# Bias tile, mask and lambda of the first attention made during the first feed-forward network, by way of DRAM

## The chip, the cores and the metric

The kernel runs on one core of one Trainium2 chip. The metric is the device time of one launch in microseconds (us), lower is better. Everything is fp32; no matrix product may lose fp32 accuracy, so each large product is made of three single-pass products of operands that are split into a high and a low part (fp32r), which is why TensorE (PE) has three kinds of rows, lines 147 to 149.

## The reference, cut to what matters

A transformer of two blocks on 256 tokens of 1024 features. The first block has two layers; in layer 0 a feed-forward network, then a differential attention, then a second feed-forward network follow each other. Only what feeds the first attention matters here:

```python
lam = exp(sum(lf[0] * lf[1])) - exp(sum(lf[2] * lf[3])) + lambda_init     # a_lambda, four vectors of 64
rel = q_pos[:, None] - k_pos[None, :]
bias = table[t5_bucket(rel)]                                             # rel_bias: 32 buckets x 8 heads
logits = q k^T * scale + bias                                            # two maps m of each of 8 heads
logits = where(rel >= 0, logits, -inf)
p = softmax(logits);  w = p[map 0] - lam * p[map 1];  o = w @ v
o = rms_norm(o, subln_g) * (1 - lambda_init)
```

The bias depends on `rel` alone, so for one head it is a Toeplitz matrix: each row is the row above it, moved by one column. Neither the bias nor `lam` depends on the activations; all they need are the small inputs `rel_bias`, `a_lambda` and a one-hot table `t5` of the bucket of each distance.

## The kernel before, in words

**Weights.** All weights stream from DRAM in chunks of 1 MB, `raw` [128, 2048] (line 105, three buffers, loaded by the DMA queue of SyncE, called SP). ScalarE (ACT) writes the high part `whi` of each half (line 115), VectorE (DVE) the low part `wlo` (line 116), four buffers each; PE multiplies them with the activations (`hi`, `lo`). A second stream `araw` (line 355, two buffers, the same queue) feeds the modulation vectors, whose products DVE makes by itself (line 358) in the background, one step every so many chunks.

**Order.** The Python text is written in program order; a scheduler then decides the order in which each engine gets its instructions. Each engine takes its own list strictly in order. Tiles that share an address wait for one another through semaphores, and so do the buffers of a tile.

**Stages around the change.** First the keys and values of a memory (`w_xk`, `w_xv`). Then the first feed-forward network (`ffn(0, ...)`): 22 chunks `ffn_in`, each giving two products, a SiLU on ACT and a split, and then 11 chunks `ffn_out`. Then the first attention: four groups `g` of two heads, in each the projections `a_q`, `a_k` and `a_v` of the next chunk and then `a_head` of two heads. GpSimd (POOL) does little: sums of squares (line 193) in the second half of the feed-forward network and some memsets.

**The bias tile.** `TB` [128, 8, 256] holds the negated bias of a head, mask included, as one Toeplitz tile; line 523 adds it to the logits. Before, it is made inside the attention, when group 0 has its projections:

```python
pe.matmul(pf, rb, oh, start=True, stop=True)                                       # L582: 8 heads x 384 distances
dve.scalar_tensor_tensor(gneg, pf, -1.0, mrow, op0=ALU.mult, op1=ALU.add)          # L584
for hd in range(8):                                                                # L588: row p is gneg moved by p
    sync.dma_start(out=TF[:, hd, :], in_=bass.AP(tensor=s_.tensor, offset=s_.offset,
                                                 ap=[list(s_.ap[0]), [1, 128], [1, 256]]))
a_v(0)
pe.matmul(pb, flip, TF[:, 2 * q:2 * q + 2, :], start=True, stop=True)              # L610, four times
act.activation(TB[:, 2 * q:2 * q + 2, :], pb, AF.Copy)                             # L611
```

Each transfer of line 588 reads one SBUF partition (one head's 384 values) 128 times over, 1 KB each time with the start moved by one value, and writes 128 partitions. The result has its rows in the wrong order, so that a product with a flipped unit matrix turns it round (line 610, plain fp32, two passes each). `nlam` (lines 599 to 605) and `g08` (line 607) are made beside it.

Of the kernel before, what the change touches and what calls it, by code (L numbers as in the profile page):

```python
# [10 lines left out]
F32 = mybir.dt.float32  # L11
# [8 lines left out]
T = 256  # L20
# [10 lines left out]
# ---- columns of the packed per-feature vectors: name -> (first column, count)  # L31
# [22 lines left out]
def forward(ctx: ExitStack, tc: tile.TileContext, io, out, tap=None):  # L54
# [21 lines left out]
    # ---------------------------------------------------------------- constants  # L76
# [15 lines left out]
    # ---------------------------------------------------------------- weights  # L92
    class Weights:
        """Streams [128, 2048] chunks; each gives two pieces split exactly into hi + lo."""
# [5 lines left out]
        def pieces(self, src, n=2048, whole=(), loads=1):  # L100
            """whole: pieces that stay plain fp32, for PE's own (slower) fp32 product."""
# [23 lines left out]
    def after(ref):  # L125
        """keeps background work from running ahead of its place in the queue."""
        return tc.issue_after(ref[0].ins) if ref[0] is not None else nullcontext()
# [17 lines left out]
    def mm3(o, a, b, start, stop):  # L145
        """o += a.T @ b for operands split into (hi, lo)."""
# [4 lines left out]
    def tok(h, k, a=0, b=T):  # L151
        """tokens a .. b of feature tile k."""
        return h[0][:, k, a:b], h[1][:, k, a:b]
# [4 lines left out]
    def split_into(pair_hi, pair_lo, src, func=AF.Copy, **kw):  # L158
        """exact hi + lo of src (an fp32 SBUF tile)."""
# [3 lines left out]
    # ---------------------------------------------------------------- norms  # L163
    class Stat:
        """Sum of squares over the features: tokens on partitions, then 1 / rms again along the row."""
# [7 lines left out]
        def sum(self, sq, first, last_):  # L173
            # the first product also clears the other half of the bank
# [27 lines left out]
        def rstd_after(self, r1):  # L202
            """1 / rms of the rows that r1 scales."""
# [7 lines left out]
    def along_row(r):  # L211
        """[token, 2] -> the same values along the tokens of every partition."""
# [9 lines left out]
    class Norm:  # L222
        """h = (src * a) * r + b in hi + lo, in place of src * a, which the first products take:
        they need no r, which is multiplied into what they give (two more columns carry b)."""
# [21 lines left out]
        def pair(self, p0, p1, keep=None):  # L246
            """two output tiles [128, T] in SBUF; then h is what it should be."""
# [29 lines left out]
    def fm_pair(p0, p1, h):  # L277
        """two feature-major output tiles [128, T]; k outermost."""
# [15 lines left out]
    def proj_fm(W, name, h, consume, c0=0, c1=None, whole=(), h32=None, ahead=None, norm=None, wide=False):  # L294
        """feature-major projection: consume(n, psum) for each output tile n.
        norm: h is still to be scaled; wide: h is only just coming."""
# [334 lines left out]
    if tap:  # L631
        tap("x_attn0", xT)
# [670 lines left out]
```

## Time and profile before

| | |
|---|---|
| device time, three runs | 2295.49, 2296.33, 2296.72 us (median 2296.33) |
| span of the profiled execution, first to last instruction | 2292.8 us |
| profiled span below the median of the runs | 3.6 us |
| mean clock of PE | 0.991 of full speed |
| PE busy | 2235.5 us |

The profile shows one execution; of its time beside the span the record gives nothing more, so that the difference of 3.6 us to the median holds both what lies around the span and what differs between runs. "Idle before" in a row of the trace is the time for which an engine had nothing to do ahead of that instruction, with what ended it. PEld is the loading of PE's stationary operand, SPq the queue of SyncE. Busy shares of PE come from modelled ends of pipelined products, so the time between the starts of two products is a better measure than their durations.

### The profile page before, as it was taken

The page shows a single profiled execution, that of the slowest core. Times are in us where ns is not written, and L with a number is a line of the kernel's source. Part 1 is how long each engine was busy: PE and PEld are TensorE (multiplying, and loading weights), DVE is VectorE, ACT ScalarE, POOL GpSimd, SP SyncE. Part 2 cuts the span into 40 slices and gives each one's busy share as a digit, 9 for nine tenths or more (in the row PEclk, how much of TensorE's full clock was granted, in tenths as well). Part 3 has the DMA queues.
Part 4 walks back from the last instruction along what each step waited for, and adds up shares of the span by engine and source line. Part 5 has one row for each costly group of instructions (what it writes and reads, how often), then busy time and mean ns, then how long its engine had stood idle before and what let it go on. Part 6 is the DMA issues. An engine that isn't in the chain of part 4 may idle for free.

```text
span 2292.8 us, 42711 instructions
## 1 busy us (share of the span) xinstructions
PE 2235.5 (98%) x16756; PEld 2133.5 (93%) x16756; DVE 1739.7 (76%) x3503; ACT 1257.1 (55%) x2389; POOL 72.0 (3%) x75
## 2 busy tenths in 40 slices
PE   8999869999999999999999999999999999999998
PEld 8999858999999999999999999999999999888886
DVE  7877727977877777855699886899668998666665
ACT  5544538644564447644533455545567776555554
POOL 0000100100200010100100000000000000000000
PEclk9999979999999999999999999999999999999999
DMA  9777664677667773455444543245543444555554
GB/s 367 297 295 294 208 138 170 234 299 279 230 266 297 293 292 129 169 202 183 167 164 166 184 181 151 95 184 184 184 166 132 145 148 148 184 190 194 185 185 155
DMA packets 66489, 466.15 MB, mean 203 GB/s; under 512 B 7472, under 2 KB 8944, under 8 KB 10480
## 3 DMA queue, kind: packets, MB, share of 16 engines
q1 hardware_dynamic: 66000, 462.90, 55.4%
q8 instruction: 132, 2.16, 0.4%
q14 instruction: 69, 0.57, 0.1%
q10 hardware_dynamic: 288, 0.52, 0.1%
HBM read 461.26 MB, written 1.05 MB: 202 GB/s over the span
## 4 chain that ended last, share of the span: by engine, by line
PE 90%; DVE 3%; ACT 3%; issue 1%; SPq 1%; DMA 1%; POOL 0%; DVEq 0%; ACTq 0%; POOLq 0%
PE mm L149 22%; PE mm L147 22%; PE mm L148 22%; PE mm L1164 8%; PE lg L1164 8%; PE lg L1114 2%; PE mm L289 2%; SPq L588 1%; PE po L177 1%; DVE wlo L116 1%; ACT whi L115 1%; DMA TF<-gneg 1%; DVE lo L275 0%; DVE lo L238 0%; DVE nt L270 0%
## 5 line engine op out<-in xcount | busy, mean ns | idle before, releaser
L116 DVE TENSOR_TENSOR wlo<-raw,whi 128x1024 fp32r<-128x1024 f32 x696 | 850.1, 1226 | 325.2 <-ACT whi L115 323.7
L115 ACT ACTIVATE whi<-raw 128x1024 fp32r<-128x1024 f32 x696 | 734.3, 1059 | 617.9 <-PE mm L148 411.9
L147 PE MATMUL mm<-hi,whi 128*128 128x256 f32 x3144 | 899.3, 287 | 0.9 <-ACT hi L274 0.6
L149 PE MATMUL mm<-hi,wlo 128*128 128x256 f32 x3144 | 891.7, 284 | 1.4 <-DVE wlo L116 1.1
L148 PE MATMUL mm<-lo,whi 128*128 128x256 f32 x3144 | 886.1, 282 | 0.6 <-DVE lo L275 0.5
L149 PEld LDWEIGHTS mm<-hi,wlo 128*128 128x128 f32 x3144 | 595.4, 189 | 3.0 <-DVE wlo L116 2.7
L148 PEld LDWEIGHTS mm<-lo,whi 128*128 128x128 f32 x3144 | 595.6, 189 | 2.6 <-DVE lo L275 1.2
L147 PEld LDWEIGHTS mm<-hi,whi 128*128 128x128 f32 x3144 | 594.4, 189 | 2.6 <-ACT hi L274 0.8
L149 PE MATMUL mm<-ghi,wlo 128*128 128x256 f32 x704 | 197.7, 281 | 0.0
L147 PE MATMUL mm<-ghi,whi 128*128 128x256 f32 x704 | 197.7, 281 | 0.0
L148 PE MATMUL mm<-glo,whi 128*128 128x256 f32 x704 | 197.7, 281 | 0.0
L358 DVE CUSTOM_DVE_ANT_0 araw<-araw,cb 128x1024 f32<-128x1024 f32 x160 | 190.3, 1218 | 1.0 <-ACT cb L407 1.0
L160 ACT ACTIVATE vph<-S 128x128 fp32r<-128x128 f32 x256 | 77.1, 302 | 133.0 <-PE lg L1164 132.9
L148 PEld LDWEIGHTS mm<-glo,whi 128*128 128x128 f32 x704 | 132.8, 189 | 0.0
L147 PEld LDWEIGHTS mm<-ghi,whi 128*128 128x128 f32 x704 | 132.8, 189 | 0.0
L149 PEld LDWEIGHTS mm<-ghi,wlo 128*128 128x128 f32 x704 | 132.8, 189 | 0.0
L161 DVE TENSOR_TENSOR vpl<-S,vph 128x128 fp32r<-128x128 f32 x256 | 73.5, 288 | 44.3 <-PE lg L1164 44.2
L812 DVE SCALAR_TENSOR_TENSOR cfc<-cf,vec,cfc 128x256 f32<-128x256 f32 x240 | 99.1, 472 | 0.0
L1106 DVE TENSOR_SCALAR ohA<-cst,sel 128x128 f32<-128x128 f32 x256 | 82.2, 342 | 21.8 <-PE lg L1114 20.9
L1164 PE MATMUL mm<-whi,vph 128*128 128x512 f32 x256 | 80.3, 395 | 0.2 <-ACT vph L160 0.2
L1164 PE MATMUL lg<-whi,vpl 128*128 128x512 f32 x256 | 80.5, 395 | 0.0
L1164 PE MATMUL mm<-wlo,vph 128*128 128x512 f32 x256 | 80.5, 395 | 0.0
(387 smaller groups left out, 3279.7 us busy)
## 6 DMA issues: line engine op xcount, KB each, us to landing
raw<-ffn_in SPq DMA_DIRECT2D x88, 1024.0 KB, 4.8
araw<-ada SPq DMA_DIRECT2D x72, 1024.0 KB, 6.8
raw<-peer_u SPq DMA_DIRECT2D x64, 1024.0 KB, 4.8
raw<-peer_v SPq DMA_DIRECT2D x64, 1024.0 KB, 4.8
raw<-ffn_out SPq DMA_DIRECT2D x44, 1024.0 KB, 4.8
araw<-kv_ada SPq DMA_DIRECT2D x8, 1024.0 KB, 6.9
raw<-w_cf SPq DMA_DIRECT2D x8, 1024.0 KB, 4.8
raw<-w_scx SPq DMA_DIRECT2D x8, 1024.0 KB, 4.8
```

Of the source, the lines that this page charges most:

```text
L115: act.activation(hi[:, :m], r, AF.Copy)
L116: last_split[0] = dve.tensor_tensor(lo[:, :m], r, hi[:, :m], op=ALU.subtract)
L147: pe.matmul(o, a[0], b[0], start=start, stop=False)
L148: pe.matmul(o, a[0], b[1], start=False, stop=False)
L149: pe.matmul(o, a[1], b[0], start=False, stop=stop)
L160: act.activation(pair_hi, src, func, **kw)
L161: dve.tensor_tensor(pair_lo, src, pair_hi, op=ALU.subtract)
L289: pe.matmul(o, p[0][:, k * 128:(k + 1) * 128], h32[:, k, :], start=(k == 0), stop=(k == KT - 1))
L358: dve.tensor_tensor_reduce(out=raw[:, i, :], in0=raw[:, i, :], in1=cb, scale=1.0, scalar=0.0, op0=ALU.mult, op1=ALU.add, accum_out=acc[:, ...
L812: dve.scalar_tensor_tensor(o, cf[:, i, j:j + T], w, o, op0=ALU.mult, op1=ALU.add)
L1106: dve.tensor_scalar(A, iota, sel3[:, 0, t:t + 1], sel3[:, 2, t:t + 1], op0=ALU.is_equal, op1=ALU.mult)
L1164: pe.matmul(acc[t][d], lh, rh[:, d * 512:(d + 1) * 512], start=s0, stop=s1)
```

## The change

`TB`, `nlam` and `g08` are made while the first feed-forward network runs, in a generator `prepare_bias` that is moved on at four places: ahead of the network (three small loads, now on POOL's queue, and two memsets), ahead of its chunks 4 and 6, and behind it. The eight transfers from one partition each and the four flips are gone. Instead POOL's queue writes the 8 rows of `mrow` 128 times over into a DRAM tile `rows` [8, 128, 384] in one transfer, and reads it back in a second one with a row pitch of 383 values, one less than a row has, which moves each row by one and puts the rows in the right order. `ohi`, which shared its address with `TF`, gets its own.

```diff
+    ask = ExitStack()
+    tbp = ask.enter_context(tc.tile_pool(name="tb", bufs=1))
+    dram = ask.enter_context(tc.tile_pool(name="dr", bufs=1, space=bass.MemoryType.DRAM))
+    TB = tbp.tile([128, 8, 256], F32, name="TB")
...
+    def prepare_bias():
+        oh = tbp.tile([32, 384], F32, name="oh")
+        rb = tbp.tile([32, 8], F32, name="rb")
+        lamb = tbp.tile([128, 4, 64], F32, name="lamb")
+        la = io["a_lambda"]
+        pool.dma_start(out=oh, in_=io["t5"])
+        pool.dma_start(out=rb, in_=io["rel_bias"])
+        pool.dma_start(out=lamb, in_=bass.AP(tensor=la.tensor, offset=la.offset, ap=[[0, 128], [64, 4], [1, 64]]))
+        mrow = tbp.tile([8, 384], F32, name="mrow")
+        pool.memset(mrow[:, 0:256], 0.0)
+        pool.memset(mrow[:, 256:384], BIG)
+        yield
+        pf = bank("lg", [8, 384])
+        pe.matmul(pf, rb, oh, start=True, stop=True)
+        dve.scalar_tensor_tensor(mrow, pf, -1.0, mrow, op0=ALU.mult, op1=ALU.add)
+        rows = dram.tile([8, 128, 384], F32, name="rows")
+        pool.dma_start(out=rows, in_=mrow.unsqueeze(1).to_broadcast([8, 128, 384]))
+
+        pool.dma_start(out=TB, in_=bass.AP(tensor=rows.tensor, offset=rows.offset + 127,
+                                           ap=[[383, 128], [128 * 384, 8], [1, 256]]))
+        yield
+        lj = tbp.tile([128, 64], F32, name="lj")
+        ls = tbp.tile([128, 2], F32, name="ls")
+        for i in range(2):
+            dve.tensor_tensor_reduce(out=lj, in0=lamb[:, 2 * i, :], in1=lamb[:, 2 * i + 1, :], scale=1.0,
+                                     scalar=0.0, op0=ALU.mult, op1=ALU.add, accum_out=ls[:, i:i + 1])
+        dve.tensor_scalar(g08, v("a_subln_g"), 1.0 - LAM0, None, op0=ALU.mult)
+        yield
+        act.activation(ls, ls, AF.Exp)
+        dve.tensor_tensor(nlam, ls[:, 1:2], ls[:, 0:1], op=ALU.subtract)
+        dve.tensor_scalar(nlam, nlam, -LAM0, None, op0=ALU.add)
+        yield
...
             for j in range(FKT):
+                if f == 0 and j in (4, 6):
+                    next(beside)
                 it = W.pieces(src[j])
...
             if g == 0:
-                oh = ap_.tile([32, 384], F32, tag="w", name="oh", bufs=2)
-                rb = ap_.tile([32, 8], F32, name="rb")
-                sync.dma_start(out=oh, in_=io["t5"])
-                sync.dma_start(out=rb, in_=io["rel_bias"])
-                mrow = ap_.tile([8, 384], F32, tag="wT", name="mrow", bufs=2)
-                pool.memset(mrow[:, 0:256], 0.0)
-                pool.memset(mrow[:, 256:384], BIG)
-                pf = bank("lg", [8, 384])
-                pe.matmul(pf, rb, oh, start=True, stop=True)
-                gneg = ap_.tile([8, 384], F32, tag="w", name="gneg", bufs=2)
-                dve.scalar_tensor_tensor(gneg, pf, -1.0, mrow, op0=ALU.mult, op1=ALU.add)
-                TF = ap_.tile([128, 8, 256], F32, tag="ohi", name="TF")
-                for hd in range(8):
-                    s_ = gneg[hd:hd + 1, :]
-                    sync.dma_start(out=TF[:, hd, :],
-                                   in_=bass.AP(tensor=s_.tensor, offset=s_.offset,
-                                               ap=[list(s_.ap[0]), [1, 128], [1, 256]]))
                 a_v(0)
...
-                for q in range(4):
-                    pb = bank("lg", [128, 2, 256])
-                    pe.matmul(pb, flip, TF[:, 2 * q:2 * q + 2, :], start=True, stop=True)
-                    act.activation(TB[:, 2 * q:2 * q + 2, :], pb, AF.Copy)
-                ohi = ap_.tile([128, 8, 256], F32R, tag="ohi", name="ohi")
```

The text says where the generator is moved on; the scheduler says where its instructions come to stand. Three places matter.

PE, before, in the second half of the chunk `a_v` 1 (`whi`, `wlo` are now the moving weights, `hi`, `lo` the stationary tokens; in brackets what each waits for, DMAHW being transfers):

```order
L147 MATMUL mm<-whi,hi 128x256 [waits Activation_49]
L148 MATMUL mm<-wlo,hi 128x256
L610 MATMUL lg<-TF,cst 128x512 [waits DMAHW7_49,DMAHW6_49,PE_49]
L149 MATMUL mm<-whi,lo 128x256
L610 MATMUL lg<-TF,cst 128x512 [waits DMAHW1_49,DMAHW0_49]
L147 MATMUL mm<-whi,hi 128x256
L148 MATMUL mm<-wlo,hi 128x256
L610 MATMUL lg<-TF,cst 128x512 [waits DMAHW3_49,DMAHW2_49,Activation_49]
L149 MATMUL mm<-whi,lo 128x256
L610 MATMUL lg<-TF,cst 128x512 [waits DMAHW5_49,DMAHW4_49,Activation_49]
L147 MATMUL mm<-whi,hi 128x256
L148 MATMUL mm<-wlo,hi 128x256
```

PE, with the change, at the same place:

```order
L147 MATMUL mm<-whi,hi 128x256 [waits Activation_49]
L148 MATMUL mm<-wlo,hi 128x256 [waits DVE_49]
L149 MATMUL mm<-whi,lo 128x256
L147 MATMUL mm<-whi,hi 128x256 [waits Activation_49]
L148 MATMUL mm<-wlo,hi 128x256
```

The four flips, each of which waited for two of the eight transfers, are gone; the products of `a_v` follow each other.

PE, with the change, at the start of the first feed-forward network, among the products of its first chunk (the scheduler put the product of bias and one-hot table, line 504, 11 products into the network, far ahead of chunk 4; before, nothing stood there):

```order
L147 MATMUL mm<-hi,whi 128x256 [waits Activation_49]
L148 MATMUL mm<-lo,whi 128x256
L504 MATMUL lg<-oh,rb 8x384 [waits DMAHW0_49,DMASW1_49,DMAHW2_49,DMASW0_49,PE_49]
L147 MATMUL mm<-hi,whi 128x256 [waits Activation_49]
L147 MATMUL mm<-hi,whi 128x256
```

Line 504 waits for the loads of `oh` and `rb` (DMASW0 and DMASW1), and every product behind it waits with it.

POOL, with the change, from the program's start to its first sum of squares (before, that sum was its first work):

```order
L496 DMA oh<-t 32x384 [waits DMAHW0_49,DVE_49,DMAHW2_49,PE_49,Activation_49]
L497 DMA rb<-rel_bias 32x8
L498 DMA lamb<-a_lambda 128x256
L500 MEMSET mrow 8x256
L501 MEMSET mrow 8x128
L507 DMA rows<-mrow 1024x1x384 [waits DVE_49]
L509 DMA TB<-rows 128x8x256 [waits DMASW3_49]
L193 ISA
L193 TENSOR_TENSOR sqa<-sq 128x256 [waits Activation_49]
```

The new tiles lie where the memory's tiles lay, so the load of `oh` waits (PE_49) for the last product of `w_xv`. The read into `TB` waits for `rows` to have landed, and the sums of squares stand behind it. On SP's queue the eight transfers of line 588 and the three small loads are gone; on ACT the exponential of lambda (line 519) now stands among the first chunks of the network, with a table load ahead of it and one behind it to return to SiLU, and the heads of group 0 have a table load of their own, as those of the other groups had before.

## Rows read from the trace of the kernel before

**Rows 1.** Page, part 1: busy time of each engine (share of span), instructions.

```profile
PE 2235.5 (98%) x16756; PEld 2133.5 (93%) x16756; DVE 1739.7 (76%) x3503; ACT 1257.1 (55%) x2389; POOL 72.0 (3%) x75
```

**Rows 2.** Waits, whole span: engine, line, releaser; total us, times, longest.

```profile
ACT whi L115 <- PE mm L148: 411.9, 317, 4.3
...
PEld lg L610 <- issue: 28.8, 4, 7.8
...
PE lg L610 <- DMA TF<-gneg: 26.5, 4, 7.6
```

**Rows 3.** Windows: length, busy of each engine, PE clock, DMA share, GB/s.

```profile
66.70:195.00 128.30, 126.64 (x1046) 125.37 (x1045) 103.63 (x157) 65.53 (x99) 0.00 (x0) 1.00 0.76 289
195.00:259.50 64.50, 64.50 (x544) 64.45 (x543) 50.36 (x66) 30.74 (x40) 6.48 (x7) 1.00 0.76 289
...
280.16:317.37 37.21, 10.67 (x23) 5.38 (x22) 3.51 (x5) 3.29 (x5) 0.00 (x0) 0.54 0.81 78
```

**Rows 4.** Timeline of PE, 279.8 to 317.5 us: start, duration, instruction, idle before.

```profile
280.04 0.27 PE L148 MATMUL mm<-wlo,hi 128*128 128x256 f32 x1
286.59 2.05 PE L610 MATMUL lg<-TF,cst 128*128 128x512 f32 x2 [6.27 <-DMA TF<-gneg]
287.64 1.20 PE L149 MATMUL mm<-whi,lo 128*128 128x256 f32 x1
...
317.19 0.34 PE L148 MATMUL mm<-wlo,hi 128*128 128x256 f32 x1
317.37 0.28 PE L149 MATMUL mm<-whi,lo 128*128 128x256 f32 x1
```

**Rows 5.** Timeline of SP's queue, 258 to 335 us.

```profile
274.09 27.80 SPq L588 DMA_DIRECT2D TF<-gneg  x8
301.99 4.96 SPq L105 DMA_DIRECT2D raw<-a_v  x1
```

**Rows 6.** Line 588: transfers, ns min/median/max of an issue.

```profile
L588 SPq DMA_DIRECT2D TF<-gneg x8: 584/4522/5011, 274.1 to 296.9; - x8
```

**Rows 7.** DMA of 100 to 190 us: packets, MB, share of 16 engines; issues, landing.

```profile
q1 hardware_dynamic: 3638, 26.52, 78.1%
...
raw<-ffn_in SPq DMA_DIRECT2D x13, 1024.0 KB, 4.8
```

**Rows 8.** Timelines of SP, ACT, DVE in a steady stretch of the first network.

```profile
95.40 0.33 SPq L105 DMA_DIRECT2D raw<-ffn_in  x1
98.80 1.06 ACT L115 ACTIVATE whi<-raw 128x1024 fp32r<-128x1024 f32 x1 [1.55 <-PE mm L148]
99.89 1.23 DVE L116 TENSOR_TENSOR wlo<-raw,whi 128x1024 fp32r<-128x1024 f32 x1 [0.43 <-ACT whi L115]
107.41 1.06 ACT L115 ACTIVATE whi<-raw 128x1024 fp32r<-128x1024 f32 x1 [1.50 <-issue]
```

**Rows 9.** PE where the first network starts, and at line 582.

```profile
66.45 0.28 PE L149 MATMUL mm<-whi,mlo 128*128 128x256 f32 x1
...
70.65 0.28 PE L148 MATMUL mm<-lo,whi 128*128 128x256 f32 x1
...
272.12 0.81 PE L582 MATMUL lg<-oh,rb 32*8 32x384 f32 x2
```

**Rows 10.** The small loads: issue on SP's queue, landing; a slow small load.

```profile
259.21 0.34 SPq L576 DMA_DIRECT2D oh<-t  x1
...
oh<-t SPq DMA_DIRECT2D x1, 48.0 KB, 2.3
...
fb<-fgate_b SPq DMA_DIRECT2D x1, 0.1 KB, 3.8
```

**Rows 11.** A table load on ACT, DVE's background step, a sum of POOL.

```profile
269.73 1.28 ACT L602 ACT_TABLE_LOAD   x1
...
282.24 1.22 DVE L358 CUSTOM_DVE_ANT_0 araw<-araw,cb 128x1024 f32<-128x1024 f32 x1
...
213.42 1.20 POOL L193 TENSOR_TENSOR sqa<-sq 128x256 f32<-128x256 f32 x1 [212.98 <-ACT sq L182]
```

More of the change, by code (lines that the diff above doesn't have):

```diff
@@ L478, in norm_of @@
         return Norm(mod(sc), mod(sh))
+    ask = ExitStack()
+    tbp = ask.enter_context(tc.tile_pool(name="tb", bufs=1))
+    dram = ask.enter_context(tc.tile_pool(name="dr", bufs=1, space=bass.MemoryType.DRAM))
+    TB = tbp.tile([128, 8, 256], F32, name="TB")
+    nlam = tbp.tile([128, 1], F32, name="nlam")
+    g08 = tbp.tile([128, 1], F32, name="g08")
+    def prepare_bias():
[29 more added lines that the diff above has]
+        yield
     norm = norm_of("0_sc1", "0_sh1")
     norm.scale(r=st.rstd())
+    beside = prepare_bias()
+    next(beside)
     st, norm = ffn(0, norm, "0_gt1", lambda: norm_of("0_sc2", "0_sh2"), done=True)
@@ L484, in forward @@
         tap("x_ffn0", xT)
+    next(beside)
     rate[0] = 0.4
@@ L489, in forward @@
         V = ap_.tile([128, 2, D], F32, name="V")
-        TB = ap_.tile([128, 8, 256], F32, name="TB")
+        ohi = ap_.tile([128, 8, 256], F32R, name="ohi")
         olo = ap_.tile([128, 8, 256], F32R, name="olo")
@@ L591, in forward @@
-                a_v(0)
-                lamb = ap_.tile([128, 4, 64], F32, name="lamb")
-                la = io["a_lambda"]
-                sync.dma_start(out=lamb, in_=bass.AP(tensor=la.tensor, offset=la.offset, ap=[[0, 128], [64, 4], [1, 64]]))
-                lj = ap_.tile([128, 64], F32, name="lj")
-                ls = ap_.tile([128, 2], F32, name="ls")
-                for i in range(2):
-                    dve.tensor_tensor_reduce(out=lj, in0=lamb[:, 2 * i, :], in1=lamb[:, 2 * i + 1, :], scale=1.0,
-                                             scalar=0.0, op0=ALU.mult, op1=ALU.add, accum_out=ls[:, i:i + 1])
@@ L601, in forward @@
-                le = ap_.tile([128, 2], F32, name="le")
-                act.activation(le, ls, AF.Exp)
-                nlam = ap_.tile([128, 1], F32, name="nlam")
-                dve.tensor_tensor(nlam, le[:, 1:2], le[:, 0:1], op=ALU.subtract)
-                dve.tensor_scalar(nlam, nlam, -LAM0, None, op0=ALU.add)
-                g08 = ap_.tile([128, 1], F32, name="g08")
-                dve.tensor_scalar(g08, v("a_subln_g"), 1.0 - LAM0, None, op0=ALU.mult)
-                for q in range(4):
-                    pb = bank("lg", [128, 2, 256])
-                    pe.matmul(pb, flip, TF[:, 2 * q:2 * q + 2, :], start=True, stop=True)
-                    act.activation(TB[:, 2 * q:2 * q + 2, :], pb, AF.Copy)
@@ L630, in forward @@
         proj_fm(W, "a_w_o", (ohi, olo), lambda n, o: residual(n, o, s[:, n:n + 1], st, norm))
+    ask.close()
     if tap:
```

## Prediction

> **What bounds the kernel now.** The page first: PE is busy for 98% of the span [rows 1], so a change pays only where PE stands still, or is slowed. The list of waits then says where PE stands still for long: nearly everything in it is an engine that waits for PE (the splits of the weights, 411.9 us in 317 waits), and the one place where PE itself waits in tens of us is line 610, the flips, for the transfers of line 588 [rows 2]. Windows by stage show what this is worth: in the first feed-forward network PE starts a product each 64.50 / 544 = 0.119 us at full clock; in the 37 us from 280.16 on it has 23, its clock falls to 0.54, DVE and ACT do next to nothing, and the DMA engines are 0.81 busy though they move 78 GB/s where the network moves 289 [rows 3]. PE's timeline gives the ends of the stall: the last product before it starts at 280.04, the next at full pace at 317.37, and between them stand four pairs of flips and 12 ordinary products, the first at 287.64, the last at 317.19 [rows 4]. SP's queue says why: it is at the eight transfers from 274.09 for 27.8 us [rows 5], 4.52 us each in the middle [rows 6], and a transfer is 128 x 1 KB out of one partition: 131 KB / 4.52 us = 29 KB per us. So this stage is bound by transfers that read a single partition each, and nothing covers them.
>
> **What is removed.** The flips' wait, the flips and the slow clock go together: without them the 13th product after 280.04 would start at 280.04 + 13 x 0.119 = 281.6, not at 317.37 [rows 4]. That is **35.8 us**, all on PE's path. What could be late next in its place: the low halves of the next chunk. DVE does two background steps from 282.24 on, 1.22 us each [rows 11], so it is at the next `wlo` at 284.7 and done at 285.9 (1.23 us [rows 8]). PE's order has 43 products of `a_v` 1 left at 280.16, which end at 285.3, then the first logits and two products with the high half, and only then one that needs that `wlo`; it fits if these take 0.6 us or more. I take a loss of 0.5 us, between nothing and 3 (both background steps and some splits in the way). The weights of the following chunks no longer stand behind line 588 on SP's queue, where one was issued at 301.99 [rows 5], so they come earlier. The copies to `TB` on ACT go as well; nothing waited for them but this stage.
>
> **What is added on PE.** The product of bias and table (line 582, 0.81 us [rows 9]) costs the same where it stands now. New is its wait. The load of `oh` can't start before the last product of `w_xv`, which starts at 66.45 and ends at 66.7 [rows 9]. On SP's queue an issue took 0.34 us and `oh` landed 2.3 us after it [rows 10]; two issues and a landing give 66.7 + 0.7 + 2.3 = 69.7. PE comes to line 504 at about 70.6, where its 12th product of the network started before [rows 9]: nothing is lost, if POOL's queue is as quick as SP's. The trace has no transfer of POOL's. Above, I take 1.2 us an issue, the longest that a sum took POOL [rows 11], and the slow landing of another small load, 3.8 us [rows 10]: 66.7 + 2.4 + 3.8 = 72.9, a loss of 2.3 us. I take 1 us. All of PE's work stands behind that row, so later loads would cost their whole delay.
>
> **What is added elsewhere.** Two table loads more in the network, 1.28 us each [rows 11], and an exponential: ACT is busy for 65.5 of 128.3 us there [rows 3], and its splits wait for PE to free a buffer (1.55 us ahead of one [rows 8]), so they are hidden; without that cover 2.8 us. The table load at the heads of group 0 lengthens one chain beside PE's products; 0.3 us. Lambda's two DVE steps and the bias row only move from a full stretch of DVE to one where it is busy for 103.6 of 128.3 us.
>
> **The two new transfers.** `rows` moves 1024 x 1.5 KB out of 8 partitions, `TB` 1024 x 1 KB out of DRAM. Both must be done by the first logits at about 286. A half of a chunk takes 2.87 us in the network (8.61 us for three [rows 8]), so chunk 4 begins at about 66.7 + 8 x 2.87 = 89.7; they start near there, and even 150 us would do. The question is what they do to the weights, which share the DMA engines. In the network each of 16 engines has 3638 / 16 = 227 packets in 90 us, one each 0.396 us, busy for 78.1% of it: 0.309 us a packet [rows 7]. If a packet of `rows` of length p goes between every two, the stream falls behind by 0.309 + p - 0.396 us each time, if that is above zero. The stream has some time in hand: a load issued at 95.40 is used by ACT at 107.41 and lands in 4.8 us, so 7.2 us to spare; the split that ACT starts at 98.80 is ready at 101.1, when DVE is through, and PE uses it three halves later, at 107.4: 6.3 us more [rows 7, 8]. Only a lag above **13.5 us** reaches PE.
> What is p? Below: the price that weights pay by the byte, 0.309 us for 7.3 KB, so 0.065 us: 0.374 is under 0.396, no lag. Above: all eight rows through at what one partition gave, 29 KB per us [rows 6]: 1573 / 29 = 54 us for `rows`. On eight engines that is 0.42 us a packet, 128 packets each, and a lag of 0.337 x 128 = 43 us, of which PE loses 29.6; on 16 engines 0.85 us, 64 packets, a lag of 48.5, a loss of 35. The nearest row is line 588's, the same kind of read, but it has one partition at a time and `rows` has eight to read side by side. With two such streams p is 0.21 and the lag 16 us, a loss of 2.4; with four, 0.11, a lag of 2, no loss. I take 1 us for it, and keep 0 and 35. `TB` by the weights' price takes 64 x 0.043 = 2.8 us of each engine, which the time in hand covers.
>
> A rule speaks against this transfer. What the rows show is 29 KB per us from one partition with the engines of that stretch 0.81 busy [rows 3, 6]. The Trainium skill, "DMA: Bandwidth & Descriptors", section "Rules for kernel authors", says that an outermost dimension of size c under 16 confines a transfer to at most c engines, which here is 8 (the partitions of `mrow`); and "SBUF — State Buffer", section "Door 1: The DMA port swizzle", that partitions 0 to 3 share one port and 4 to 7 another. By these two pages the transfer would be two streams on eight engines, the ground of the first rival below, and with packets that alternate the sum would be 1.4 us worse than mine. The trace agrees with a limit of one partition's port; no run here shows two partitions read at once.
>
> **The sum.** -35.8 + 0.5 (DVE) + 1 (wait at line 504) + 0.3 (table) + 1 (`rows`) = -33.0. From the profiled span, 2292.8 - 33.0 = 2259.8; the median of the runs stands 3.6 us above that span, so **2263.3 us**. Own range: no loss at all gives 2260.5, less 2 for an order of instructions that differs through the rest of the program; with 2.3 at line 504, 3 at DVE and 2.4 for `rows` it is 2268. So 2258 to 2268.
>
> **The rivals.**
> *The gain is given back in part.* `rows` holds half the DMA engines and the splits run dry some 20 to 60 us after it starts. For: the engines are 78% busy already [rows 7], and a queue need not alternate packet by packet. If it sends longer runs, the lag is at most all the time that two streams need, 27 us, and PE loses up to 27 - 13.5 = 13.5. Against: the time in hand. Time 2268 to 2277, say 2272. Chance 0.17.
> *The gain is nearly all given back.* One stream for all eight rows on eight engines, a loss of 29.6: 2291; or the loads of `oh` and `rb` come late by tens of us, with PE behind line 504. Against: eight partitions, and 3.8 us for the slowest small load [rows 10]. 2280 to 2291. Chance 0.05.
> *No change.* The change doesn't do what it says: PE would have stood still at 280 for something else, the splits of DVE, say. Against: of these 37 us DVE works 3.5 and ACT 3.3 [rows 3]. Or all but 4 us of the gain go as above. 2292 to 2301. Chance 0.03.
> *Slower.* The same collision in the network, with every packet of `rows` at more than the price of one stream on 16 engines: the lag passes 13.5 + 34 + 4.6 us when p is above 0.90 us (0.309 + 0.90 - 0.396 = 0.81, times 64, is 52); one stream gives 0.85 [rows 6]. With p of 1 us the lag is 58, the loss 45, and the time 2296 - 34 + 45 = 2307. For: a second reader on the ports that the weights are written through is not in any row. Against: eight partitions. Chance 0.04.
>
> **The numbers.** The forecast itself has 0.71. Faster by over 0.2% (4.6 us, about what a measurement of this kernel can tell from no change) takes the forecast and the first two rivals: 0.93; the same 0.03; slower 0.04. The range for 8 in 10 goes from 2258 over the forecast's own and most of the first rival to 2277: 0.71 + 0.15.
>
> **What would show it.** Right: no wait of PE above 2 us between 279 and 320, PE's clock at full speed there; SP's loads of `a_v` and `a_q` issued a chunk apart; in the network a product of PE each 0.12 us as now, with a DMA share near 1 for a while after the bias row. Wrong: waits of PE for `whi` or `wlo` in the network, with ACT waiting for `raw`; a wait of PE at line 504 above 3 us; loads of `raw` that land in 10 us; DVE waiting for `araw`; or `TB` landing after the first logits. The forecast falls if `rows` is read slower than two partitions' worth, or if POOL takes several us to issue its first loads.

## Result and profile after

The changed kernel took **2271.78 us** (median of 4 runs, 2270.45 to 2273.96) beside 2296.07 for the kernel before: a ratio of 0.9897 [0.9884, 0.9909]. Measured a second time, beside the last experiments, it took 2266.41 us (2264.82 to 2267.72) beside 2295.27: 0.9876 [0.9861, 0.9891]. It is faster by 24 to 29 us, where 33 were forecast. The first measurement lies above the forecast of 2263.3 and above its own range (2258 to 2268), the second inside that range; the whole range (2258 to 2277) holds both, and 2272 is the time that the first rival gave.

The first profile has a span of 2271.2 us, 21.6 less than before. Its windows, with the columns of [rows 3], in the first network and where the flips stood:

```profile
66.00:72.00 6.00, 4.70 (x26) 2.96 (x24) 3.70 (x9) 4.81 (x10) 2.16 (x5) 0.90 0.16 32
72.00:80.00 8.00, 8.00 (x46) 7.77 (x46) 6.98 (x13) 2.15 (x4) 0.00 (x0) 0.65 0.92 345
...
110.00:120.00 10.00, 7.16 (x60) 6.95 (x59) 1.18 (x2) 0.00 (x0) 0.00 (x0) 1.00 0.88 244
120.00:131.00 11.00, 7.03 (x40) 7.03 (x41) 4.06 (x5) 2.69 (x4) 0.00 (x0) 0.69 0.66 188
131.00:140.00 9.00, 6.87 (x45) 6.67 (x44) 6.36 (x11) 5.28 (x8) 0.93 (x1) 0.81 0.91 337
...
280.00:290.00 10.00, 10.00 (x84) 9.83 (x83) 9.90 (x24) 7.18 (x15) 0.00 (x0) 1.00 0.42 178
290.00:300.00 10.00, 10.00 (x86) 10.00 (x85) 9.37 (x14) 6.25 (x10) 0.00 (x0) 1.00 0.75 286
```

From 280 on PE is never idle and its clock is full, where it had 23 products in 37 us [rows 3]. But the network, which had run at full pace, now has a hole: from 110 to 140 us PE has 60 + 40 + 45 = 145 products, and the kernel before had 259 there. That is 114 products, 13 us at 8.6 a microsecond. A second, smaller loss stands at the network's start, where the clock is 0.65 from 72 to 80.

POOL's timeline (start, duration, instruction, idle time before it) gives two marks, the transfers and the first sum of squares, which comes when the first network's first half is done:

```profile
91.74 1.08 POOL L507 DMA_DIRECT2D rows<-mrow  x1 [21.40 <-DVE mrow L505]
131.05 0.93 POOL L509 DMA_DIRECT2D TB<-rows  x1 [38.23 <-DMA rows<-mrow]
230.32 1.20 POOL L193 TENSOR_TENSOR sqa<-sq 128x256 f32<-128x256 f32 x1 [98.34 <-ACT sq L182]
```

That sum started at 213.42 before [rows 11], so up to here the change has lost 16.9 us. The next first sum, behind the attention, comes 152.80 us later (383.12), where it was 190.65 before: 37.85 us won. The rest of the program is 0.65 us shorter: -37.85 + 16.9 - 0.65 = -21.6, the whole difference of the spans.

The list of waits from 60 to 240 us (engine, line, releaser; total us, times, longest):

```profile
POOL TB L509 <- DMA rows<-mrow: 38.2, 1, 38.2
...
ACT whi L115 <- DMA raw<-ffn_in: 27.4, 5, 12.7
...
PEld mm L147 <- ACT sil L450: 9.8, 3, 7.0
```

The splits on ACT wait for weights 27.4 us, which is no row of the list before, and PE waits for a SiLU. How the one comes of the other stands in the timelines of ACT and of PE:

```profile
122.59 1.06 ACT L115 ACTIVATE whi<-raw 128x1024 fp32r<-128x1024 f32 x1 [12.71 <-DMA raw<-ffn_in]
123.55 0.36 ACT L450 ACTIVATE sil<-mm 128x256 f32<-128x256 f32 x1
```

```profile
116.88 0.28 PE L149 MATMUL mm<-hi,wlo 128*128 128x256 f32 x1
123.97 0.58 PE L147 MATMUL mm<-hi,whi 128*128 128x256 f32 x1 [6.81 <-ACT sil L450]
```

ACT has had nothing since 109.88; when the weights come at 122.59 it does the split, then the SiLU behind it, and only then is PE's next bank free. The first products after that run at half clock (0.58 us in place of 0.28). On SP's queue the loads go out as forecast, the next `a_q` at 277.52 and the next `a_v` at 294.13, with no line 588 ahead of them.

### The profile page after: what moved, and what is told of

The parts are those of the page before. It is cut to its first block, busy times and chain, and to the rows that moved or that the text cites. A ratio compares the mean times of both kernels' runs of the same rounds, so it can differ in the third digit from the quotient of the medians.

```text
span 2271.2 us, 42683 instructions
## 1 busy us (share of the span) xinstructions
PE 2230.7 (98%) x16748; PEld 2132.8 (94%) x16748; DVE 1739.8 (77%) x3503; ACT 1256.8 (55%) x2387; POOL 75.5 (3%) x80
## 4 chain that ended last, share of the span: by engine, by line
PE 91%; DVE 3%; ACT 3%; DMA 2%; issue 1%; POOL 0%; DVEq 0%; ACTq 0%; POOLq 0%
PE mm L149 22%; PE mm L147 22%; PE mm L148 22%; PE mm L1172 8%; PE lg L1172 8%; PE lg L1122 2%; PE mm L289 2%; DMA raw<-ffn_in 1%; PE po L177 1%; DVE wlo L116 1%; ACT whi L115 1%; DVE lo L238 0%; DVE lo L275 0%; ACT e L572 0%; PE po L958 0%
## 5 line engine op out<-in xcount | busy, mean ns | idle before, releaser
L147 PEld LDWEIGHTS mm<-hi,whi 128*128 128x128 f32 x3144 | 597.1, 190 | 13.3 <-ACT sil L450 10.1
L1114 DVE TENSOR_SCALAR ohA<-cst,sel 128x128 f32<-128x128 f32 x256 | 82.4, 343 | 21.7 <-PE lg L1122 20.7
L1172 PE MATMUL lg<-whi,vph 128*128 128x512 f32 x256 | 80.5, 395 | 0.0
```

The costliest lines, as they stand in the source:

```text
L147: pe.matmul(o, a[0], b[0], start=start, stop=False)
L1114: dve.tensor_scalar(A, iota, sel3[:, 0, t:t + 1], sel3[:, 2, t:t + 1], op0=ALU.is_equal, op1=ALU.mult)
L1172: pe.matmul(acc[t][d], lh, rh[:, d * 512:(d + 1) * 512], start=s0, stop=s1)
```

## Experiments

Each edit is to the changed kernel unless it says otherwise. The measured numbers of all runs stand together first; each ratio, with its 95% interval, is to the kernel before, beside which it ran; it is taken from all runs and can differ from the quotient of the medians by up to 0.0008. "Landing" is the time of `rows` from issue to landing, "first sum" the mark at 230.32 above (213.42 in the kernel before).

| run | median us | ratio | landing us | first sum |
|---|---|---|---|---|
| changed kernel | 2271.78 | 0.9897 [0.9884, 0.9909] | 39.0 | 230.32 |
| changed kernel, second time | 2266.41 | 0.9876 [0.9861, 0.9891] | 38.5 | 225.84 |
| no transfers | 2257.79 | 0.9835 [0.9822, 0.9849] | none | 214.70 |
| copies from DRAM | 2258.71 | 0.9841 [0.9827, 0.9854] | 10.6 | 214.60 |
| heads four partitions apart | 2260.29 | 0.9847 [0.9833, 0.9860] | 25.4 | 214.74 |
| heads two apart | 2259.64 | 0.9848 [0.9835, 0.9861] | 25.1 | 216.98 |
| control, partitions 0 to 7 | 2270.09 | 0.9895 [0.9879, 0.9910] | 37.9 | 224.85 |
| ACT's queue | 2266.37 | 0.9875 [0.9860, 0.9890] | about 40 | 224.15 |
| 16 senders | 2261.02 | 0.9852 [0.9838, 0.9865] | 20.6 | 218.17 |
| line 504 held | 2267.13 | 0.9874 [0.9859, 0.9889] | 37.3 | 223.19 |
| copies from DRAM, 504 held | 2258.04 | 0.9842 [0.9828, 0.9855] | 12 | 215.44 |
| four apart, 504 held | 2260.00 | 0.9849 [0.9834, 0.9864] | 21.7 | 215.24 |
| two halves | 2264.60 | 0.9874 [0.9859, 0.9889] | 20.5, 21.4 | 219.89 |

**Is it the transfers?** The first run leaves both out.

```diff
-        rows = dram.tile([8, 128, 384], F32, name="rows")
-        pool.dma_start(out=rows, in_=mrow.unsqueeze(1).to_broadcast([8, 128, 384]))
-
-        pool.dma_start(out=TB, in_=bass.AP(tensor=rows.tensor, offset=rows.offset + 127,
-                                           ap=[[383, 128], [128 * 384, 8], [1, 256]]))
+        pool.memset(TB, 0.0)
```

> The two transfers of lines 507 and 509 are left out and TB is filled with zeros by POOL, so the attention's logits lack their bias and mask; all else of the change stays (product at line 504, bias row, lambda, table loads). Theory A (the transfer of `rows` takes the DMA engines from the weights, and that costs the network 13 us): PE starts a product each 0.12 us from 100 to 140 us, the first sum of squares of POOL (end of the network's first half, at 230.3 in the changed kernel) comes at about 217, and the time is 2271.8 - 13 = 2259, 2256 to 2262 with the order of the rest. Rival B (the wait at line 504, the table loads of ACT or lambda's steps cost the network its time): 2268 or more, PE as slow at 110 to 140 us as now.

2257.79 us. Its windows and its first sum:

```profile
110.00:120.00 10.00, 10.00 (x85) 10.00 (x85) 8.33 (x12) 4.26 (x7) 0.00 (x0) 1.00 0.95 376
120.00:131.00 11.00, 11.00 (x94) 11.00 (x93) 8.03 (x12) 5.39 (x8) 0.00 (x0) 1.00 0.73 266
```

```profile
214.70 1.20 POOL L193 TENSOR_TENSOR sqa<-sq 128x256 f32<-128x256 f32 x1 [141.99 <-ACT sq L182]
```

The hole is gone, so it belongs to the two transfers: they cost 8.6 to 14.0 us, by which of the two measurements of the changed kernel one takes; the 14.0 has in it the smaller loss at the network's start, 2.6 us in the first profile, which the runs with line 504 take up. Everything else that the change adds to the network, line 504 included, costs 214.70 - 213.42 = 1.3 us.

**Is it their bytes, or where they are read?** The bias row goes to DRAM once, and the copies are made from there.

```diff
+        row = dram.tile([8, 384], F32, name="row")
+        pool.dma_start(out=row, in_=mrow)
-        rows = dram.tile([8, 128, 384], F32, name="rows")
-        pool.dma_start(out=rows, in_=mrow.unsqueeze(1).to_broadcast([8, 128, 384]))
+        rows = dram.tile([128, 8, 384], F32, name="rows")
+        pool.dma_start(out=rows, in_=row.unsqueeze(0).to_broadcast([128, 8, 384]))
...
-                                           ap=[[383, 128], [128 * 384, 8], [1, 256]]))
+                                           ap=[[8 * 384 - 1, 128], [384, 8], [1, 256]]))
```

> The bias row goes to DRAM once (8 x 1.5 KB), and the 128 copies are made from there by a transfer from DRAM to DRAM with the 128 copies outermost (128 x 12 KB, the same 1.57 MB written); TB is read as now. Theory A in the form that the source counts (eight partitions of SBUF on eight engines): spread over 16 engines by the price per byte of the weights it is 1573 / 7.3 x 0.309 / 16 = 4.2 us of each engine, less than the 13.5 us in hand: no wait of PE for whi or wlo from 100 to 140 us, `rows` lands within 15 us of its issue, 2257 to 2262. Rival C (1.5 MB through POOL's queue beside the weights costs as much from any source, by its bytes or by how that queue is served): `rows` takes 30 us or more again and the time is 2268 to 2276.

2258.71 us, `rows` lands in 10.6 us, and PE has 86 and 94 products in the two windows: the same bytes through the same queue cost nothing that can be measured. The rival with the bytes falls. The read into `TB` stands in this run too, so the loss belongs to `rows` alone.

**Is it the partitions?** The rows are read from SBUF again, but from partitions 0, 4, ... 28.

```diff
-        rb = tbp.tile([32, 8], F32, name="rb")
+        rb = tbp.tile([32, 8, 4], F32, name="rb")
+        pool.memset(rb, 0.0)
...
-        pool.dma_start(out=rb, in_=io["rel_bias"])
+        pool.dma_start(out=rb[:, :, 0], in_=io["rel_bias"])
...
-        mrow = tbp.tile([8, 384], F32, name="mrow")
+        mrow = tbp.tile([32, 384], F32, name="mrow")
...
-        pf = bank("lg", [8, 384])
-        pe.matmul(pf, rb, oh, start=True, stop=True)
+        pf = bank("lg", [32, 384])
+        pe.matmul(pf, rb.rearrange("b h r -> b (h r)"), oh, start=True, stop=True)
...
-        pool.dma_start(out=rows, in_=mrow.unsqueeze(1).to_broadcast([8, 128, 384]))
+        pool.dma_start(out=rows, in_=mrow[0:32:4, :].unsqueeze(1).to_broadcast([8, 128, 384]))
```

> The columns of rel_bias are put four apart (a 32 x 32 table with zeros between), so the bias rows of the eight heads stand in partitions 0, 4, ... 28 and not 0 to 7; the transfer of `rows` is otherwise the same, outermost dimension 8. Theory A1 (what limits it is the reading of neighbouring partitions through one or two ports): each of eight partitions gives up to 29 KB per us, `rows` lands in 10 to 20 us and the loss in the network falls from 13 to 0 to 4 us: 2258 to 2264. Theory A2 (what limits it is that only eight engines carry 128 packets each, whatever the partitions): `rows` takes 39 us as now, 2270 to 2274.

2260.29 us; `rows` takes 25.4 us, which is more than the 10 to 20 expected, and PE never runs dry. Two more runs of this form follow, with the same instructions in the same order: a control, which reads partitions 0 to 7 out of the padded tile, and one with the heads two partitions apart.

```diff
-        pool.dma_start(out=rows, in_=mrow[0:32:4, :].unsqueeze(1).to_broadcast([8, 128, 384]))
+        pool.dma_start(out=rows, in_=mrow[0:8, :].unsqueeze(1).to_broadcast([8, 128, 384]))
```

> The control of the run with heads four partitions apart: the same padded 32 x 32 table, the same instructions in the same order, but the bias rows stand in partitions 0 to 7 again. Theory A1 (neighbouring partitions share a way out): `rows` takes 37 to 40 us from issue to landing and the network loses 8 to 14 us again: 2266 to 2273. Rival (the gain of that run came from the padding, the other order or an earlier start, not from the partitions): 2258 to 2262 as with the heads four apart.

> The same, with the bias rows two partitions apart (0, 2, ... 14). Theory A1 in the form that groups of four neighbouring partitions share one way out: twice as many ways as in the control and half as many as four apart, so `rows` lands after 20 to 30 us and the loss is a few us at most: 2258 to 2264. If only direct neighbours (or all of one block of 16) count, it is as with one of the two ends: 25 us and 2260, or 39 us and 2270.

The control gives 2270.09 us and 37.9 us of landing, the hole again; two apart gives 2259.64 and 25.1. So it is the source's partitions and nothing else of the padded form. The price is in the DMA queues of 93 to 112 us (packets, MB, share of 16 engines; q1 carries the weights, q0 what POOL issues), first the kernel before, then the control, with how many of all its packets are how small, then two apart:

```profile
q1 hardware_dynamic: 790, 5.72, 78.0%
```

```profile
DMA packets 1074, 4.72 MB, mean 248 GB/s; under 512 B 407, under 2 KB 407, under 8 KB 618
q1 hardware_dynamic: 515, 3.73, 51.9%
q0 software_dynamic: 558, 0.98, 37.4%
```

```profile
q1 hardware_dynamic: 764, 5.54, 77.6%
q0 software_dynamic: 633, 1.30, 17.5%
```

The counts show what a packet is. Of the control's, 407 are under 512 B and none has 0.5 to 2 KB; the 618 - 407 = 211 of 2 to 8 KB (the kernel before has none) carry the 0.98 MB of `rows`, so 4.6 KB, or three copies, each, as the trace counts packets. The price is therefore taken by the copy, of which 0.98 MB are 638: out of partitions 0 to 7 a copy holds an engine for 0.374 x 16 x 19 / 638 = 0.178 us, and two apart for 0.175 x 16 x 19 / 846 = 0.063 us (four apart the same). With two apart the weights keep their 5.5 MB, in the control they fall to 3.7. "SBUF — State Buffer" of the Trainium skill, section "Door 1: The DMA port swizzle", puts partitions 0 to 7 on two ports, two apart on four and four apart on eight. By that rule, the trace agrees with a limit of the ports at two, and shows none between four and eight.

**Is it POOL's queue?** ACT issues the transfer instead.

```diff
-        pool.dma_start(out=rows, in_=mrow.unsqueeze(1).to_broadcast([8, 128, 384]))
+        act.dma_start(out=rows, in_=mrow.unsqueeze(1).to_broadcast([8, 128, 384]))
```

> The changed kernel with the transfer of `rows` issued by ACT instead of POOL; the source is as in the changed kernel. Theory A1 (the source's partitions, not the queue): `rows` takes 37 us or more again, PE runs dry at 110 to 140 us, 2266 to 2275 (ACT's own issue of about 1 us is covered). Rival C (POOL's queue is what takes the engines from the weights in long runs): another queue shares better, and it is 2258 to 2263.

2266.37 us, as the changed kernel's second measurement. From 93 to 112 us:

```profile
q10 hardware_dynamic: 637, 0.98, 38.1%
q1 hardware_dynamic: 352, 2.49, 36.5%
```

The new queue, q10, takes the same 38%, and it does so in packets of one copy each (0.98 MB in 637) where POOL's have three. Neither the queue nor the length of its packets is what counts.

**Is it that few engines send it?** Each row is made in two neighbouring partitions, 16 in all, and each sends 64 copies (from the form with two apart).

```diff
-            pool.dma_start(out=rb[:, 0:8, 0], in_=io["rel_bias"])
+        for i in range(2):
+            pool.dma_start(out=rb[:, 0:8, i], in_=io["rel_bias"])
...
-        pool.dma_start(out=rows, in_=mrow[0:16:2, :].unsqueeze(1).to_broadcast([8, 128, 384]))
+        pool.dma_start(out=rows.rearrange("h (s c) j -> (h s) c j", s=2),
+                       in_=mrow[0:16, :].unsqueeze(1).to_broadcast([16, 64, 384]))
```

> Each bias row is made twice, in neighbouring partitions 2h and 2h + 1 (0 to 15 in all), and each of the 16 sends 64 copies: an outermost dimension of 16 in place of 8, out of the same four groups of four partitions as the run with rows two apart, the same 1024 packets. Theory (the partitions' way out decides, the number of engines little): within 2 us of that run, and `rows` lands about as late. Rival (eight engines with 128 packets each are the limit): `rows` lands clearly earlier than with rows two apart, 15 to 20 us, at 2257 to 2260.

2261.02 us, `rows` lands 4.5 us earlier than with two apart, and the time is the same within its interval. The landing tells little: with line 504 held, a few us later in the network, the form with four apart landed 3.7 us earlier too (21.7 in place of 25.4). What a copy costs tells more. From 93 to 112 us:

```profile
q0 software_dynamic: 354, 1.57, 54.5%
q1 hardware_dynamic: 479, 3.47, 44.2%
```

Nearly all of the 1024 copies went in this stretch, at 0.545 x 16 x 19 / 1024 = 0.162 us each, nearly as much as in the control, though they come out of the same four groups of partitions as with two apart (0.063 us). The weights fall to 3.47 MB, lower than in the control; but the transfer is over in 20.6 us and not in 38, and PE never runs dry (86 and 94 products in the two windows). So neither theory holds as it was put: the groups of partitions alone do not set the price. In the two dear forms four senders share a group of four partitions (8 senders on two groups, 16 on four), in the cheap ones two or one; that this is the reason was not tested by itself.

**Is it line 504 that costs the clock?**

```diff
-        pe.matmul(pf, rb, oh, start=True, stop=True)
+        tc.keep_in_program_order(pe.matmul(pf, rb, oh, start=True, stop=True))
```

> The product of line 504 is held at its place in the code, in front of chunk 4, instead of near the network's first products; ACT, POOL and SP issue the same in the same order. Theory: the wait for `oh` (0.5 us and what goes with it) and the half clock after it, which cost 22 products or about 2.6 us between 66 and 80 us, go away: PE has some 30 products in 66 to 72 and 65 in 72 to 80 as in the kernel before, clock 1.00, and the time falls by 2 to 3 us to about 2269. Rival: the half clock from 71.5 on comes of something else at the network's start; then it stays and the time is 2271 to 2273.

2267.13 us, below the changed kernel's first measurement by 4.7 us and above its second by 0.7. Taken alone it could be told as a success; the other runs say no. In the profiles that still have the wait, the clock fell at the network's start in three (the changed kernel's first, two apart, 16 senders) and stayed full in seven; four apart, PE stood there for 1.15 us at that product, longer than the 0.55 of the changed kernel, and its clock stayed full. Two more runs settle it. They join this edit to the DRAM copies and to four apart.

> The copies made from DRAM to DRAM, and the product of line 504 held at its place ahead of chunk 4: both losses of the network taken away. Theory: PE waits for neither, its clock stays at 1.00 from 60 to 230 us, the first sum of squares of POOL comes at 213.4, as in the kernel before, and the time is 1.2 us under that of the same transfer without the hold, 2256 to 2259. Rival: the held product waits for something at its new place, or holds the bias row back: 2260 or more.

> The same hold with the bias rows four partitions apart in SBUF as the source: 2257 to 2260, no half clock between 60 and 230 us, `rows` landing in 25 us and no wait of PE at 100 to 140. If the half clock at the network's start has nothing to do with the wait at line 504, it can show up here or in the run beside it all the same.

2258.04 and 2260.00 us, the same as without the hold. Windows of two apart, of four apart and of the DRAM copies with line 504 held:

```profile
72.00:80.00 8.00, 8.00 (x48) 8.00 (x49) 5.94 (x10) 1.70 (x3) 0.00 (x0) 0.67 0.95 377
```

```profile
72.00:80.00 8.00, 7.74 (x63) 7.53 (x63) 6.94 (x13) 4.50 (x7) 0.00 (x0) 1.00 0.94 368
```

```profile
72.00:74.00 2.00, 2.00 (x11) 2.00 (x11) 2.00 (x4) 0.91 (x2) 0.00 (x0) 0.50 0.84 319
80.00:100.00 20.00, 20.00 (x163) 19.22 (x162) 18.04 (x32) 12.36 (x18) 1.06 (x2) 1.00 0.76 296
```

Two apart and four apart have the same instructions in the same order, the one at half clock and the other not; and the last of the three kernels has no wait at line 504 and yet the half clock. Held, the product costs PE about as much where it then stands: 163 products from 80 to 100 us, where 168 stood with the DRAM copies alone (0.6 us). The theory falls: the hold wins nothing that can be measured.

**Does the loss follow the time in hand?** The source stays in partitions 0 to 7, but the copies go in two transfers.

```diff
-        pool.dma_start(out=rows, in_=mrow.unsqueeze(1).to_broadcast([8, 128, 384]))
-
+        pool.dma_start(out=rows[:, 0:64, :], in_=mrow.unsqueeze(1).to_broadcast([8, 64, 384]))
+        yield
+        mrow2 = tbp.tile([8, 384], F32, name="mrow2")
+        with after(last_split):
+            dve.tensor_scalar(mrow2, mrow, 1.0, None, op0=ALU.mult)
+        pool.dma_start(out=rows[:, 64:128, :], in_=mrow2.unsqueeze(1).to_broadcast([8, 64, 384]))
...
-                if f == 0 and j in (4, 6):
+                if f == 0 and j in (4, 12, 14):
```

> The source stays in partitions 0 to 7, but the 128 copies go in two transfers of 64, the second held back by a copy of the bias row that DVE makes 16 half chunks (about 46 us) later. Theory (a lag that the weights' time in hand covers up to 13.5 us, and that is made good between transfers): each half takes about 19 us and puts the weights 7 to 10 us behind, PE runs dry in neither, 2257 to 2262. Rival (what the two groups of partitions cost reaches PE at once, in proportion to the bytes): the loss is spread but stays, 2266 to 2272.

2264.60 us (2261.88 to 2267.24), between the two theories, and its windows show each right for one half. The first half was issued at 88.57, the second at 133.85:

```profile
110.00:120.00 10.00, 10.00 (x86) 10.00 (x85) 8.81 (x14) 5.80 (x9) 0.00 (x0) 1.00 0.92 360
134.00:145.00 11.00, 11.00 (x94) 11.00 (x94) 8.29 (x13) 5.40 (x8) 0.67 (x1) 1.00 0.77 164
145.00:155.00 10.00, 9.22 (x78) 9.02 (x76) 2.89 (x5) 1.36 (x2) 0.00 (x0) 1.00 0.84 183
155.00:165.00 10.00, 6.69 (x43) 6.69 (x44) 6.62 (x10) 4.97 (x7) 0.93 (x1) 0.83 0.91 353
```

POOL's queue from 88 to 110 us, and from 134 to 156:

```profile
q0 software_dynamic: 368, 0.79, 24.2%
...
q0 software_dynamic: 368, 0.79, 40.0%
```

The first half puts no hole into PE's work, so a lag is covered up to a point and the cost is not in proportion to the bytes. The second does (43 products from 155 to 165 where 86 are the pace), with as many bytes but not at the same price: it held the engines for 0.400 x 16 x 22 = 141 us in all, the first half for 0.242 x 16 x 22 = 85. Why as many copies out of the same partitions (of a second tile) cost more the second time was not settled.

**The changed kernel once more.**

> The changed kernel once more, on the chip of the runs beside it: 2268 to 2274, `rows` 37 to 40 us from issue to landing. What the half clock after line 504 hangs on: if it always follows that wait in this program, it is there again from 71 to 78 us; if it is a matter of the single execution (three of the eight profiles with the wait had it, five did not, and the waits were as long), it can as well be missing, and the network's first sum then comes 2 to 7 us earlier than at 230.3.

2266.41 us, a little under the expected range; no half clock from 71 to 78 (65 products from 72 to 80), and the first sum 4.5 us earlier. It shows cleanly what the hole is made of. Its ACT (idle time before it in brackets), its windows, and its DMA queues of 93 to 112 us:

```profile
99.37 1.06 ACT L115 ACTIVATE whi<-raw 128x1024 fp32r<-128x1024 f32 x1
...
105.01 1.06 ACT L115 ACTIVATE whi<-raw 128x1024 fp32r<-128x1024 f32 x1 [4.28 <-DMA raw<-ffn_in]
...
115.56 1.06 ACT L115 ACTIVATE whi<-raw 128x1024 fp32r<-128x1024 f32 x1 [7.45 <-DMA raw<-ffn_in]
116.52 0.36 ACT L450 ACTIVATE sil<-mm 128x256 f32<-128x256 f32 x1
...
127.86 1.06 ACT L115 ACTIVATE whi<-raw 128x1024 fp32r<-128x1024 f32 x1 [9.21 <-DMA raw<-ffn_in]
128.82 0.36 ACT L450 ACTIVATE sil<-mm 128x256 f32<-128x256 f32 x1
```

```profile
110.00:120.00 10.00, 6.82 (x46) 6.62 (x45) 3.03 (x4) 2.69 (x4) 0.00 (x0) 0.84 0.80 223
120.00:131.00 11.00, 6.13 (x44) 5.93 (x43) 4.43 (x7) 2.74 (x5) 0.93 (x1) 0.81 0.83 272
131.00:140.00 9.00, 9.00 (x67) 9.00 (x67) 7.09 (x11) 3.87 (x6) 0.00 (x0) 0.84 0.86 320
```

```profile
q1 hardware_dynamic: 512, 3.73, 51.2%
q0 software_dynamic: 560, 0.97, 37.3%
```

PE is idle for 3.2 + 4.9 = 8.1 us. In the 21.95 us that it is busy it has 157 products, where 189 is the full pace: 32 fewer, 3.7 us more, at a clock of 0.81 to 0.84 in the mean. Together 11.8 us, beside 225.84 - 214.70 = 11.1 by the marks. PE waits for the SiLU, and the SiLU stands in ACT's order right behind a split whose weights are late.

## Why the prediction was right or wrong

**What is removed: right, and a little too small.** With line 504's loss taken off, the forecast's terms from 213 us on were -35.8 + 0.5 + 0.3 = -35.0; the marks give -37.85. No run separates the 2.8 us more; the terms for DVE and for the table at the heads are at most nothing, since PE has 84 products in the ten us from 280 and no long wait.

**Line 504: the size was right.** 1 us was taken, and without the transfers the whole start and rest of the network lost 1.3 us. The half clock that the first profile shows after it (22 products fewer than before from 66 to 80 us, 2.6 us) does not hang on this wait, since a held run has it too. Whether the change makes it more frequent stays open; the one profile of before does not have it.

**The table loads: right.** Without the transfers the two stand in the network as in the changed kernel, and PE has its full pace.

**`rows`: this term failed by its size.** "I take 1 us for it" stood in the sum; the runs give 8.6 to 14.0. Step by step, by the second profile of the changed kernel:

- The price p was about right, a little high. "With two such streams p is 0.21", and the trace has 0.373 x 16 x 19 / 632 = 0.18 us a copy (0.97 MB are 632). That a packet is one copy was wrong: POOL's queue sent three in one, as the counts of the control show.
- The time in hand was about right: 13.5 us, of which 6.3 for the splits. In the first profile PE started its last product 7.0 us after ACT had come to a stand at 109.88.
- The lag was not. The prediction let one copy of `rows` go between every two packets of the weights, which gives 16 us. ACT's sixth split from 99.37 on (those at 106.24 and 116.78 lie in the lines left out) starts at 127.86, and at 2.87 us each it would at 113.7: 14.1 us late, on top of the 7.2 in hand at the loads, so the weights came 21 us late. Less the 13.5 in hand that is 8, and PE stood for 8.1. "DMA: Bandwidth & Descriptors" of the Trainium skill, section "Rules for kernel authors", confines an outermost dimension of 8 to eight engines. By that rule, q0's 37.3% of 16 engines is 75% of each of the eight, and, if these were never idle, some five copies of `rows` went to one packet of the weights (0.75 / 0.18 beside 0.25 / 0.309); 128 x 0.18 = 23.0 us of each in 38.5 leave 15.5 for weights, where 0.78 x 38.5 = 30.0 are wanted, and (30.0 - 15.5) / 0.78 is a lag of 19 us. The trace agrees with that in size; no view here names the engines, and why the weights got so few turns stays open.
- What came behind the wait was not priced. PE's clock falls to half (1.2 GHz) after it has stood still, and that costs 3.7 us more (4.2 in the first profile: 36 products).
- The choice itself was too low: two streams, the nearest case, gave 2.4 by the prediction's own reckoning, and 1 was a mean with four streams, for which no row spoke.

**The second measurement lies in the forecast's own range by luck.** In its profile `rows` costs 11.1 us by the marks, 10.1 more than the sum had, and the rest of the network's start 0.3 more. The stall gives 2.9 us more than forecast (152.76 us between the two sums), the rest of the program 1.4, and from span to median stand 0.5 us where the forecast added 3.6: 7.4 of the 10.4 us came back from terms that have nothing to do with `rows`. Of the 3.6, half was a difference between executions: in each run of a changed form the time stands 1.8 us above its own span (2273.0 over 2271.2).

The forecast said that it falls "if `rows` is read slower than two partitions' worth". It was read at 41 KB per us, where two partitions give 58; but beside the weights, and at somewhat less than the price of two streams a copy. The mechanism is the first rival's, longer runs of `rows` than one copy between packets of the weights, as far as the shares show it: its bound of 13.5 us was the right order, and what spoke against it, "the time in hand", was there as reckoned, but not enough. The other rivals did not come. The signs named for "wrong" are the ones that showed: loads of `raw` that land in 17 to 28 us, ACT waiting for `raw`, and PE waiting for ACT.

**The better version.** Copies made from DRAM, or heads two or four partitions apart, give 2258 to 2260 us, 6 to 14 us below the changed kernel by its two measurements and 35 to 37 below the one before; they can't be told from the run without any transfer (2257.79) by more than their intervals.

## What to carry to other kernels

A transfer off the critical path is not free because its bytes are few: reckon how long it holds the engines that the critical stream needs, by the partitions that it reads, and let it win more than every second turn. Here a small broadcast was better read from DRAM, or from rows that lie some partitions apart; both edits took the loss away without moving the transfer in time. Twice the senders hardly changed the price of a copy, but halved the time for which the weights were held up, and that was enough too. And when a stream is late, look at what stands behind it in an in-order engine: here PE stopped for a SiLU, and then paid again with its clock.

## What the runs showed of the hardware

- Eight bias rows in partitions 0 to 7 gave 1573 KB in 37.9 to 39.0 us beside the weights; two or four partitions apart they took 25 us (22 in a form with line 504 held), and a copy of 1.5 KB held an engine for 0.063 us in place of 0.18.
- Sixteen senders in partitions 0 to 15 held an engine for 0.16 us a copy, as eight in partitions 0 to 7 did, and were done in 20.6 us.
- POOL's queue put three copies into a packet, ACT's one; both held 37 to 38% of 16 engines from 93 to 112 us.
- Which queue issued the transfer (POOL's or ACT's) did not change the time beyond what two measurements of the changed kernel differ by.
- PE's clock fell to half for some 3 to 7 us at the network's start in four of thirteen profiles of the changed forms, with and without the wait at line 504, in one of two kernels whose instructions stand in the same order, and in one of two profiles of the changed kernel itself.
